# Seven block products instead of eight in twelve tile pairs of the second FFN

## The chip, the cores and the metric

The kernel runs on one core of one Trainium2 chip. The metric is the device time of one execution in microseconds, lower is better. The engines are TensorE (PE, with its weight loads as PEld), VectorE (DVE), ScalarE (ACT), GpSimd (POOL) and SyncE (SP), which issues the transfers. They run in parallel, each through its own queue in the order in which the program is written for it, and meet at semaphores.

## What is computed

A trunk of two layers, 512 tokens of 1024 features: adaptive norm, a mixer (attention in the first layer, a recurrent one in the second), and a gated FFN with a causal convolution of three taps. What matters here is the FFN of the second layer:

```python
def conv_ffn(h, w_up, conv_w, w_down):
    up = causal_dwconv(h @ w_up, conv_w)
    a, b = jnp.split(up, 2, axis=-1)
    return (jax.nn.silu(a) * b) @ w_down

    h = modulate(x, norm_ffn[layer], sh2, sc2)
    x = x + g2[:, None, :] * conv_ffn(h, ffn_w_up[layer], ffn_conv[layer], ffn_w_down[layer])
```

`w_up` is 1024 x 5632 and `w_down` 2816 x 1024, all float32.

## The kernel before

**Layout.** Features lie on the 128 partitions and the 512 tokens along a row. `x` and the normed `h` are eight tiles of 128x512. A float32 operand is split in a high and a low part of the type float32r, and a product is three matmuls (`mm3`, L322 to 326): the weights' high part by the tokens' high part, by their low part, and the weights' low part by the tokens' high part. A 128x128 block of weights is the stationary operand and up to 512 tokens stream past it.

**Weights.** `prep` (L299 to 314) loads one tile of weights (`st`, 512 KB, two buffers) with SyncE, ScalarE casts it to `whi` (L312), VectorE subtracts for `wlo` (L313); `whi` and `wlo` have five buffers each. `weight` (L316 to 320) is called where a product needs its tile, and keeps two tiles of weights prepared ahead (`LA` = 2, L246). The list of all tiles in the order of use is `weight_order`.

**The FFN** (`ffn`, from L510). The 44 feature tiles of the up projection make 22 pairs: tile j (a) and tile 22 + j (b). A pair is 2 x 8 x 3 = 48 matmuls of 128x512 into two PSUM banks that `gbank` (L267 to 269) takes in turn from six. The first two pairs go by halves of the tokens, 256 wide, as the norm's two halves come. `finish` puts the pair through the convolution (`conv`, L516 to 523: one ScalarE operation and two VectorE operations from the bank), Silu, the product and a split into `gh` and `gl`.

**The down projection** sums over the 22 product tiles in three parts (`THIRDS`, L21: 0, 8, 15, 22). After pair 8 and after pair 15 all eight output tiles are made for one part, each 8 or 7 x 3 matmuls, and added to `x` (`residual`, L429). The last part is `out_gemm` (from L483): four tiles 512 wide, then four by halves.

**The norm ahead of it.** `out_gemm` of the mixer, called with a next norm, sums squares (`sq`, `stat`), and `rstd_bc` (L442 to 464) takes their sum over partitions on TensorE (L450), 1 / rms on VectorE by a chain of small operations (`nv`, `nrt`, `nry`, L455 and L351 to 356), and its broadcast on TensorE (L460, bank `t`). `make_h` (L470 to 476) then makes `hu` on VectorE, `hh` on ScalarE and `hl` on VectorE. This runs once per half of the tokens.

The order on each engine comes from the tile framework: code is written in the order above, and a scheduler places each instruction by its priority in the program.

Of the kernel before, what the change touches and what calls it, by code (L numbers as in the profile page):

```python
# [12 lines left out]
ALU = mybir.AluOpType  # L13
# [7 lines left out]
THIRDS = (0, 8, 15, 22)  # L21
# [50 lines left out]
# features of the state space layer: groups of 16 (o) for states of odd and even tiles of states  # L72
# [51 lines left out]
def layout(inp):  # L124
# [55 lines left out]
    dn = np.zeros((2, 3, 8, P, 1024), np.float32)  # L180
    for l in range(2):
        for q in range(3):
            w = wtiles(g["ffn_w_down"][l][THIRDS[q] * P:THIRDS[q + 1] * P])
            dn[l, q, :, :, :w.shape[2]] = w
    A["dn"] = dn
    A["cc"], A["ba"], A["bb"], A["id"], A["turns"], A["i16"] = constants()
    return A


def weight_order():  # L190
# [4 lines left out]
    def ffn(l):  # L195
        r = []
        for j in range(NJ):
            r += [("up", l, j), ("up", l, NJ + j)]
            if j in THIRDS[1:3]:
                r += [("dn", l, THIRDS.index(j) - 1, m) for m in range(8)]  # L200
        return r + [("dn", l, 2, m) for m in range(8)]
# [28 lines left out]
SPLIT_AT = (18, 18, 18, 18)  # L230
REC_K = (2, 3, 4, 5, 0, 1, 6, 7)


class Kernel:
    def __init__(self, nc, tc, I, O, ctx):
        self.nc, self.tc, self.I, self.O, self.ctx = nc, tc, I, O, ctx
        self.guards = {}
# [9 lines left out]
        self.turn = 0  # L247
        self.tturn = 0

# [1 line left out]
    def open(self, name, side="left"):  # L251
        p = self.tc.tile_pool(name=name, bufs=1, side=side, reuse_waits="tile")
        t = p.__enter__()
        self.guards[name] = p
        return t
# [11 lines left out]
    def gbank(self):  # L267
        self.turn = (self.turn + 1) % 6
        return self.bank(("acc", "acc", "s", "s", "o", "o")[self.turn])
# [9 lines left out]
    def source(self, key):  # L279
# [16 lines left out]
        n = (THIRDS[key[2] + 1] - THIRDS[key[2]]) * P  # L296
        return I["dn"][key[1], key[2], key[3], :, :n], n

    def prep(self, pool=None, stage=None):  # L299
        key = self.order[self.next]  # L300
        self.next += 1
        src, n = self.source(key)
# [57 lines left out]
    def ada_first(self, k, pool, V):  # L360
        """Scale and shift of a feature tile of the first norm, in three steps: loads, long sums, last sums."""
# [11 lines left out]
        if k in ADA_PE:  # L373
            # four parts of the sum side by side on the tensor engine
# [67 lines left out]
    def rstd_bc(self, stats, cs, tag="x", warm=None):  # L442
        """1 / rms of each token, on all partitions; stats: squares to be summed."""
# [26 lines left out]
    def make_h(self, l, kind, k, rs, cs):  # L470
        nc = self.nc
        u = self.sp.tile([P, T], F32, name="hu", tag="hu", bufs=2)[:, cs]
# [1047 lines left out]
```

## Time and profile before

| | us |
|---|---|
| median of three runs | 1322.74 (1322.55 to 1324.81) |
| span of the profiled execution | 1321.6 |
| TensorE busy | 1302.3 (99%) |
| weight loads busy | 1075.0 (81%) |
| VectorE busy | 910.8 (69%) |
| ScalarE busy | 576.0 (44%) |

The profiled execution's span is the time from its first to its last recorded instruction; the runs were timed apart. Busy shares are averages over stages with different limits. The second FFN ends the kernel: its first product of full width starts at 976.81, behind two pairs by halves, and the last matmul of the kernel at 1317.84.

### The profile page before, as it was taken

To read this page: it belongs to the slowest core of one execution; us is meant where nothing else is said; L and a number is where in the kernel's file an instruction comes from. 1 tells how busy PE (TensorE), PEld (TensorE's weight loads), DVE (VectorE), ACT (ScalarE), POOL (GpSimd) and SP (SyncE) were. 2 spreads that over 40 slices of the span, in tenths; PEclk is the share of its full clock that TensorE was granted. 3 is DMA by queue.
4 is the path that set the end of the run, shared out by engine and by line. 5 is a ranking of instruction groups with operands and counts; after the bars stand their busy time and mean duration, and the time that the engine had idled before them with its cause. 6 is when DMAs were issued, how large, how long until landed. Compare 5 with 4: busy or idle time off the path is not lost.

```text
span 1321.6 us, 21082 instructions
## 1 busy us (share of the span) xinstructions
PE 1302.3 (99%) x8190; PEld 1075.0 (81%) x8190; DVE 910.8 (69%) x2025; ACT 576.0 (44%) x1114; POOL 3.3 (0%) x11
## 2 busy tenths in 40 slices
PE   8989999999999999999999999999999999999998
PEld 5976776898886888888998879787998888888888
DVE  6986856579995598486678786774885644654652
ACT  4456556445531333233456655553444423432430
POOL 0000000000000000000000000000000000000000
PEclk9999999999999999999999999999999999999999
DMA  9763521516654577363443522311422222222222
GB/s 365 267 224 119 175 65 41 201 65 217 213 170 154 178 252 248 125 212 116 142 159 100 156 92 63 98 31 59 150 97 98 96 96 97 95 94 101 94 79 78
DMA packets 81971, 181.02 MB, mean 137 GB/s; under 512 B 28432, under 2 KB 36048, under 8 KB 81872
## 3 DMA queue, kind: packets, MB, share of 16 engines
q1 hardware_dynamic: 81872, 179.69, 40.4%
q8 instruction: 64, 1.05, 0.3%
q14 instruction: 35, 0.29, 0.1%
HBM read 165.55 MB, written 14.11 MB: 136 GB/s over the span
## 4 chain that ended last, share of the span: by engine, by line
PE 91%; DVE 4%; DMA 2%; ACT 2%; issue 1%; SPq 0%; DVEq 0%; ACTq 0%
PE acc L324 12%; PE acc L325 12%; PE acc L326 12%; PE s L325 7%; PE s L324 7%; PE s L326 7%; PE o L325 7%; PE o L324 7%; PE o L326 6%; PE s L646 3%; PE o L675 2%; DMA ast<-ada 1%; DVE wlo L313 1%; DVE adaj L395 1%; PE t L666 1%
## 5 line engine op out<-in xcount | busy, mean ns | idle before, releaser
L312 ACT CAST whi<-st 128x1024 fp32r<-128x1024 f32 (+1 forms) x196 | 201.1, 1029 | 291.6 <-PE acc L325 101.9
L313 DVE TENSOR_TENSOR wlo<-st,whi 128x1024 fp32r<-128x1024 f32 (+1 forms) x196 | 234.1, 1196 | 127.3 <-ACT whi L312 124.7
L324 PE MATMUL acc<-hh,whi 128*128 128x512 f32 (+1 forms) x488 | 178.9, 370 | 0.9 <-ACT hh L475 0.7
L325 PE MATMUL acc<-hl,whi 128*128 128x512 f32 (+1 forms) x488 | 178.6, 369 | 0.2 <-DVE hl L344 0.2
L326 PE MATMUL acc<-hh,wlo 128*128 128x512 f32 (+1 forms) x488 | 178.0, 367 | 0.0
L325 PE MATMUL s<-hl,whi 128*128 128x512 f32 (+2 forms) x368 | 131.1, 356 | 0.0
L324 PE MATMUL s<-hh,whi 128*128 128x512 f32 (+2 forms) x368 | 130.3, 354 | 0.0
L326 PE MATMUL s<-hh,wlo 128*128 128x512 f32 (+2 forms) x368 | 129.9, 353 | 0.0
L395 DVE CUSTOM_DVE_ANT_0 adaj<-ast,cond 128x1024 bf16<-128x1024 f32 x86 | 104.8, 1218 | 13.8 <-DMA ast<-ada 13.5
L325 PE MATMUL o<-hl,whi 128*128 128x512 f32 (+1 forms) x288 | 106.8, 371 | 0.0
L324 PE MATMUL o<-hh,whi 128*128 128x512 f32 (+1 forms) x288 | 106.7, 370 | 0.0
L326 PE MATMUL o<-hh,wlo 128*128 128x512 f32 (+1 forms) x288 | 106.1, 368 | 0.0
L324 PEld LDWEIGHTS acc<-hh,whi 128*128 128x128 f32 x488 | 91.1, 188 | 17.0 <-ACT hh L475 1.0
L325 PEld LDWEIGHTS acc<-hl,whi 128*128 128x128 f32 x488 | 91.3, 188 | 16.2 <-DVE hl L344 1.2
L326 PEld LDWEIGHTS acc<-hh,wlo 128*128 128x128 f32 x488 | 91.4, 188 | 15.2 <-issue 0.7
L325 PE MATMUL acc<-wlo,hh 128*128 128x256 f32 x320 | 93.3, 292 | 0.0
L324 PE MATMUL acc<-whi,hh 128*128 128x256 f32 x320 | 92.5, 290 | 0.6 <-ACT hh L475 0.6
L326 PE MATMUL acc<-whi,hl 128*128 128x256 f32 x320 | 91.6, 288 | 0.9 <-DVE hl L476 0.9
L324 PEld LDWEIGHTS s<-hh,whi 128*128 128x128 f32 (+1 forms) x368 | 68.3, 186 | 10.8
L326 PEld LDWEIGHTS s<-hh,wlo 128*128 128x128 f32 (+1 forms) x368 | 68.3, 186 | 10.4
L325 PEld LDWEIGHTS s<-hl,whi 128*128 128x128 f32 (+1 forms) x368 | 68.3, 186 | 9.9
L324 PEld LDWEIGHTS acc<-whi,hh 128*128 128x128 f32 x320 | 60.4, 189 | 4.9 <-issue 3.2
(439 smaller groups left out, 2593.5 us busy)
## 6 DMA issues: line engine op xcount, KB each, us to landing
ast<-ada SPq DMA_DIRECT2D x92, 512.0 KB
st<-up SPq DMA_DIRECT2D x88, 512.0 KB
st<-dn SPq DMA_DIRECT2D x32, 448.0 KB
st<-ri SPq DMA_DIRECT2D x20, 512.0 KB
st<-wq SPq DMA_DIRECT2D x17, 512.0 KB
st<-dn SPq DMA_DIRECT2D x16, 512.0 KB
st<-wo SPq DMA_DIRECT2D x8, 512.0 KB
st<-ro SPq DMA_DIRECT2D x8, 512.0 KB
```

The lines of the kernel that those rows point to most:

```text
L312: nc.scalar.copy(hi, st)
L313: nc.vector.tensor_tensor(lo, st, hi.bitcast(F32), ALU.subtract)
L324: mm(out, lh, rh, start=start, stop=False)
L325: mm(out, lh, rl, start=False, stop=False)
L326: mm(out, ll, rh, start=False, stop=stop)
L395: self.nc.vector.tensor_tensor_reduce(junk, st, self.cond, 1.0, 0.0, op0=ALU.mult, op1=ALU.add, accum_out=self.md[l][:, i:i + 1])
L646: nc.tensor.matmul(sb, qT[pr, i * P:(i + 1) * P], kT[pr, j0 * P:(i + 1) * P], start=True, stop=True)
L666: nc.tensor.transpose(tb[:, j * P:(j + 1) * P], ps[par][:, j * P:(j + 1) * P], self.ident)
L675: nc.tensor.matmul(ob[64 * par:64 * par + 64, i * P:(i + 1) * P], V[:, j0 + j, vc:vc + 64], pts[:, par, j * P:(j + 1) * P], start=j == 0, ...
```

## The change

In the second layer's FFN twelve of the 22 pairs (5, 6, 8, 9, 11, 12, 14, 15, 17, 18, 20, 21) are made by Strassen's scheme in Winograd's form. A pair is seen as a 2 x 2 block product: the weights' two feature tiles (a, b) by the two halves of the 1024 inner features, and the tokens' two halves of 256 by the same. Eight block products become seven, each 4 inner tiles x 3 = 12 matmuls of 128x256, 84 in all. Their operands are sums of blocks:

- `prep_pair` loads both tiles of weights of a pair, splits a's two blocks and one of b, makes four sums of blocks on VectorE (128x512) and splits those too: three casts and subtractions of 1024 and one of 512, where two of 1024 were. The buffers `v` have a ring of two.
- `token_sums` makes four sums of the tokens' blocks once, at the entry of the FFN. For that the norm's `hu` tiles are kept (`hk`) and get their shift on ScalarE.
- `seven` makes the products into three banks Z, X, Y, and adds on in PSUM where it can: the order is Z, X, Z, X, Z, Y, Z. Between them ScalarE copies what Z and X held (`p1`, `p7`, `p16`, 128x256) to SBUF, and VectorE and ScalarE make the results `ub` and `ua` there, from which `conv` then reads.

The parts of the down projection in this FFN are (0, 6, 12, 17, 22), four instead of three, and their tiles are spread one or two behind each pair from 6 on (`down_after`). In this FFN the banks go round by eight. `conv` takes its temporaries from the buffers `sq` and `stat`.

```diff
-THIRDS = (0, 8, 15, 22)
+GROUPS = ((0, 8, 15, 22), (0, 6, 12, 17, 22))
+FAST = ((), tuple(j for j in range(4, 22) if j % 3 != 1))
+SPREAD = (False, True)
...
+def down_after(l, j):
+    g = GROUPS[l]
+    q = max(n for n, b in enumerate(g) if b <= j)
+    if q == 0:
+        return []
+    if not SPREAD[l]:
+        return [(q - 1, m) for m in range(8 if j == g[q] else 0)]
+    n, i = g[q + 1] - g[q], j - g[q]
+    return [(q - 1, m) for m in range(8 * i // n, 8 * (i + 1) // n)]
...
+    def prep_pair(self, l, j):
+        pool = (self.wp, self.fp)[j % 2]
+        a, b = (pool.tile([P, 1024], F32, name="st", tag="st", bufs=2) for _ in range(2))
+        nc.sync.dma_start(a, self.I["up"][l, j])
+        nc.sync.dma_start(b, self.I["up"][l, NJ + j])
+        def halves(src, pool, tag, bufs):
+            n = src.shape[1]
+            hi, lo = (pool.tile([P, n], F32R, name=tag + e, tag=tag + e, bufs=bufs) for e in ("hi", "lo"))
+            nc.scalar.copy(hi, src)
+            nc.vector.tensor_tensor(lo, src, hi.bitcast(F32), ALU.subtract)
+            return [(hi[:, c:c + T], lo[:, c:c + T]) for c in range(0, n, T)]
+        f["11"], f["12"] = halves(a, self.wp, "w", 5)
+        f["22"], = halves(b[:, T:], self.fp, "v", 2)
+        a1, a2, b1, b2 = a[:, :T], a[:, T:], b[:, :T], b[:, T:]
+        nc.vector.tensor_tensor(b2, b2, b1, ALU.add)
+        nc.vector.tensor_tensor(b1, b1, a1, ALU.add)
+        nc.vector.tensor_tensor(a1, a1, b2, ALU.add)
+        f["s3"], f["s1"] = halves(b, self.wp, "w", 5)
+        nc.vector.tensor_tensor(a2, a2, a1, ALU.add)
+        f["s2"], f["s4"] = halves(a, self.wp, "w", 5)
...
     def weight(self, key):
-        while self.next < min(ix + (self.LA if ix > 5 else 0) + 1, len(self.order)):
+        ahead = (1 if key[0] == "sp" else self.LA) if ix > 5 else 0
+        if key[0] == "sp" and self.order[min(ix + 1, len(self.order) - 1)][0] == "dn":
+            ahead = 2
+        while self.next < min(ix + ahead + 1, len(self.order)):
...
+    def token_sums(self, l, tp):
+        for k in range(KD):
+            h = self.keep[k]
+            nc.scalar.activation(h, h, AF.Identity, bias=self.shift(l, 1, k))
+        for k in range(4):
+            h, g = self.keep[k], self.keep[k + 4]
+            V_.tensor_tensor(a, h[:, t1], h[:, t2], ALU.subtract)
+            V_.tensor_tensor(c, g[:, t2], h[:, t2], ALU.subtract)
+            V_.scalar_tensor_tensor(b, a, -1.0, g[:, t2], ALU.mult, ALU.subtract)
+            V_.scalar_tensor_tensor(d, b, -1.0, g[:, t1], ALU.mult, ALU.subtract)
+            for e, (n, m) in enumerate((("1", "3"), ("2", "4"))):
+                hi, lo = self.split(s[e], *(tp.tile([P, T], F32R, name=f"b{k}{e}{x}") for x in "hl"))
...
+    def seven(self, f, B, tp):
+        Z, X, Y = (self.gbank()[:, t1] for _ in range(3))
+        def product(acc, a, b, start):
+            for k in range(4):
+                s = slice(k * P, (k + 1) * P)
+                (lh, ll), (rh, rl) = f[a], B[b][k]
+                for n, (x, y) in enumerate(((lh, rh), (lh, rl), (ll, rh))):
+                    nc.tensor.matmul(acc, x[:, s], y, start=start and k == n == 0, stop=k == 3 and n == 2, skip_group_check=not start)
+        product(Z, "11", "11", True)
+        p1 = keep(Z, "p1")
+        product(X, "s3", "3", True)
+        p7 = keep(X, "p7")
+        product(Z, "s2", "2", False)
+        p16 = keep(Z, "p16")
+        product(X, "22", "4", False)
+        V_.scalar_tensor_tensor(v[:, t1], X, -1.0, p16, ALU.mult, ALU.subtract)
+        product(Z, "s1", "1", False)
+        V_.scalar_tensor_tensor(v[:, t2], Z, -1.0, p7, ALU.mult, ALU.subtract)
+        product(Y, "12", "21", True)
+        V_.tensor_tensor(u[:, t1], Y, p1, ALU.add)
+        product(Z, "s4", "22", False)
+        S_.copy(u[:, t2], Z)
```

**TensorE, in pair 8.** In the rows, `o_11022` and `o_11053` are the banks of the pair's two tiles before, `hh` and `hl` the normed tokens, `whi` and `wlo` the weights. Before, at the step from the first tile to the second:

```order
L324 MATMUL o_11022<-hh7_10091,whi_10949 128x512
L325 MATMUL o_11022<-hl7_10092,whi_10949 128x512
L326 MATMUL o_11022<-hh7_10091,wlo_10950 128x512
L324 MATMUL o_11053<-hh0_10077,whi_10980 128x512
L325 MATMUL o_11053<-hl0_10078,whi_10980 128x512
L326 MATMUL o_11053<-hh0_10077,wlo_10981 128x512
```

After, at the step from the second product (X is `o_11277`) to the third, which goes into Z (`o_11276`) again; the `b` tiles are the sums of tokens:

```order
L606 MATMUL o_11277<-b30h_10366,whi_11197 128x256
L606 MATMUL o_11277<-b30l_10367,whi_11197 128x256
L606 MATMUL o_11277<-b30h_10366,wlo_11198 128x256
L606 MATMUL o_11276<-b01h_10328,whi_11202 128x256
L606 MATMUL o_11276<-b01l_10329,whi_11202 128x256
L606 MATMUL o_11276<-b01h_10328,wlo_11203 128x256
```

Where a new bank began, the product now goes on in a bank that held an earlier one, of which ScalarE has taken a copy in between.

**ScalarE, in pair 9.** Before, casts of weights stand between the operations of a pair's convolution and its split; here pair 7 (`s_10946` and `s_10977` are its banks), and it goes on so in all pairs:

```order
L312 CAST whi_11056<-st_11054 128x1024
L520 ACTIVATE ta_11008<-s_10946,pc_70 128x512
L527 ACTIVATE ta_11008<-ta_11008 128x512
L312 CAST whi_11101<-st_11099 128x1024
L520 ACTIVATE tb_11013<-s_10977,pc_70 128x512
L343 CAST gh_11018<-tb_11013 128x512
L312 CAST whi_11133<-st_11131 128x1024
```

After, around the three copies of pair 9 (`acc_11465` is its Z, `s_11466` its X); `vhi_11644` and `st_11637` belong to pair 11, `whi_11436` to a down tile and `whi_11461` to pair 10:

```order
L327 CAST whi_11410<-st_11390 128x1024
L359 CAST whi_11436<-st_11434 128x768
L393 CAST gh_11385<-tb_11380 128x512
L359 CAST whi_11461<-st_11459 128x1024
L610 COPY p1_11482<-acc_11465 128x256
L327 CAST vhi_11644<-st_11637 128x512
L610 COPY p7_11496<-s_11466 128x256
L610 COPY p16_11510<-acc_11465 128x256
L359 CAST whi_11581<-st_11579 128x1024
L650 ACTIVATE tb_11569<-ub_11469,pc_70 128x512
```

The three copies stand among the casts of later weights, one of them behind a cast of a tile of pair 11.

**VectorE, at the entry of the FFN.** The chain of `nv`, `nrt` and `nry` for the second half of the tokens. Before:

```order
L455 TENSOR_SCALAR nv_10261<-x_10258 128x2
L313 TENSOR_TENSOR wlo_10333<-st_10330,whi_10332 128x1024
L351 TENSOR_SCALAR nrt_10264<-nv_10261 128x2
L352 TENSOR_SCALAR nry_10263<-nrt_10264 128x2
L354 TENSOR_TENSOR nrt_10264<-nry_10263 128x2
L355 SCALAR_TENSOR_TENSOR nrt_10264<-nrt_10264,nv_10261 128x2
L356 SCALAR_TENSOR_TENSOR nry_10263<-nrt_10264,nry_10263 128x2
```

After (`vlo_10784` and `st_10776` belong to pair 5):

```order
L505 TENSOR_SCALAR nv_10264<-x_10261 128x2
L328 TENSOR_TENSOR vlo_10784<-st_10776,vhi_10783 128x512
L401 TENSOR_SCALAR nrt_10267<-nv_10264 128x2
L335 TENSOR_TENSOR st_10776<-st_10776 128x512
L402 TENSOR_SCALAR nry_10266<-nrt_10267 128x2
L336 TENSOR_TENSOR st_10776<-st_10776,st_10775 128x512
L404 TENSOR_TENSOR nrt_10267<-nry_10266 128x2
L405 SCALAR_TENSOR_TENSOR nrt_10267<-nrt_10267,nv_10264 128x2
L360 TENSOR_TENSOR wlo_10389<-st_10386,whi_10388 128x1024
L406 SCALAR_TENSOR_TENSOR nry_10266<-nrt_10267,nry_10266 128x2
```

Three operations of 512 of pair 5's weights have moved in between the steps, beside the one subtraction of a weight that stood there.

## Rows read from the trace of the kernel before

**Rows 1.** The page: busy time, share and instructions; chain that ended last.

```profile
PE 1302.3 (99%) x8190; PEld 1075.0 (81%) x8190; DVE 910.8 (69%) x2025; ACT 576.0 (44%) x1114; POOL 3.3 (0%) x11
...
PE 91%; DVE 4%; DMA 2%; ACT 2%; issue 1%; SPq 0%; DVEq 0%; ACTq 0%
```

**Rows 2.** Busy time by window: from:to and length, engines' busy us (instructions), clock, DMA.

```profile
1000.00:1100.00 100.00, 100.00 (x439) 82.05 (x438) 52.84 (x61) 32.05 (x40) 0.00 (x0) 1.00 0.27 95
```

**Rows 3.** Timeline (start, length, engine, line): TensorE's run of full width; the end.

```profile
976.81 0.39 PE L324 MATMUL o<-hh,whi 128*128 128x512 f32 x1
...
1298.17 0.28 PE L324 MATMUL o<-gh,whi 128*128 128x256 f32 x1
...
1317.84 0.28 PE L326 MATMUL acc<-gh,wlo 128*128 128x256 f32 x1
1318.15 0.48 DVE L429 SCALAR_TENSOR_TENSOR x<-acc,mb,x 128x256 f32<-128x256 f32 x1 [1.99 <-PE acc L326]
```

**Rows 4.** Waits from 880 us on (total, times, longest): TensorE's longest; ScalarE's casts.

```profile
PE s L1188 <- DVE z L1183: 0.6, 1, 0.6
...
ACT whi L312 <- PE acc L325: 41.0, 21, 4.4
```

**Rows 5.** A window of 256 wide products only; one group of weight loads from 1298.2 on.

```profile
930.00:940.00 10.00, 10.00 (x87) 10.00 (x86) 7.05 (x12) 4.41 (x7) 0.00 (x0) 1.00 0.44 150
...
L325 PEld LDWEIGHTS o<-gl,whi 128*128 128x128 f32 x28 | 5.3, 188 | 0.0
```

**Rows 6.** Groups of VectorE (count, busy, mean ns): second FFN; last from 880 to 977.

```profile
L313 DVE TENSOR_TENSOR wlo<-st,whi 128x1024 fp32r<-128x1024 f32 x46 | 56.3, 1225 | 56.7 <-ACT whi L312 55.5
L313 DVE TENSOR_TENSOR wlo<-st,whi 128x896 fp32r<-128x896 f32 x16 | 17.4, 1090 | 21.1 <-ACT whi L312 21.1
L529 DVE TENSOR_TENSOR tb<-ta,tb 128x512 f32<-128x512 f32 x21 | 14.5, 692 | 0.8
L521 DVE SCALAR_TENSOR_TENSOR ta<-s,pc,ta 128x511 f32<-128x511 f32 x7 | 5.2, 744 | 0.0
L429 DVE SCALAR_TENSOR_TENSOR x<-acc,mb,x 128x512 f32<-128x512 f32 x8 | 5.9, 750 | 19.7 <-PE acc L326 19.7
...
L429 DVE SCALAR_TENSOR_TENSOR x<-o,mb,x 128x256 f32<-128x256 f32 x4 | 1.9, 480 | 1.4 <-PE o L326 1.4
```

**Rows 7.** Groups of ScalarE: second FFN; the last one, a copy from PSUM, whole kernel.

```profile
L312 ACT CAST whi<-st 128x1024 fp32r<-128x1024 f32 x45 | 47.1, 1048 | 81.3 <-PE acc L325 27.8 <-PE s L325 27.4 <-PE o L325 22.3
L343 ACT CAST gh<-tb 128x512 fp32r<-128x512 f32 x22 | 13.7, 620 | 56.2 <-DVE tb L529 56.2
L520 ACT ACTIVATE tb<-s,pc 128x512 f32<-128x512 f32 x8 | 5.5, 685 | 0.0
...
L667 ACT COPY PT<-x 128x256 f32<-128x256 f32 x16 | 6.0, 373 | 5.7 <-PE x L666 5.5
```

**Rows 8.** One load of weights: SyncE's issue, then windows with the DMA share.

```profile
1045.03 0.33 SPq L309 DMA_DIRECT2D st<-dn  x1
...
1045.75:1046.00 0.25, 0.25 (x3) 0.21 (x2) 0.25 (x1) 0.00 (x0) 0.00 (x0) 1.00 0.10 16
...
1047.75:1048.00 0.25, 0.25 (x3) 0.19 (x2) 0.14 (x1) 0.08 (x1) 0.00 (x0) 1.00 0.31 82
```

**Rows 9.** Timeline of VectorE: the chain to 1 / rms of the second half.

```profile
958.24 0.16 DVE L455 TENSOR_SCALAR nv<-x 128x2 f32<-128x2 f32 x1
958.32 1.21 DVE L313 TENSOR_TENSOR wlo<-st,whi 128x1024 fp32r<-128x1024 f32 x1
959.45 0.16 DVE L351 TENSOR_SCALAR nrt<-nv 128x2 int32<-128x2 int32 x1
...
961.41 0.16 DVE L356 SCALAR_TENSOR_TENSOR nry<-nrt,nry 128x2 f32<-128x2 f32 x1
```

**Rows 10.** Timeline behind it: TensorE's broadcast; ScalarE's hh, two tiles a row.

```profile
961.80 0.60 PE L460 MATMUL t<-ident,nry 128*128 128x128 f32 x4
...
962.96 0.91 ACT L475 ACTIVATE hh<-hu,mb 128x256 fp32r<-128x256 f32 x2 [5.43 <-DVE hu L474]
...
964.81 0.91 ACT L475 ACTIVATE hh<-hu,mb 128x256 fp32r<-128x256 f32 x2 [0.94 <-DVE hu L474]
```

More of the change, by code (lines that the diff above doesn't have):

```diff
@@ L197, in ffn @@
         for j in range(NJ):
[L198 to L201, printed above, removed]
+            r += [("sp", l, j)] if j in FAST[l] else [("up", l, j), ("up", l, NJ + j)]
+            r += [("dn", l, q, m) for q, m in down_after(l, j)]
+        return r + [("dn", l, len(GROUPS[l]) - 2, m) for m in range(8)]
     o += ffn(0)
@@ L254, in open @@
         self.guards[name] = p
+        self.guarded[name] = t
         return t
@@ L301, in prep @@
         self.next += 1
+        if key[0] == "sp":
+            self.ready[key] = self.prep_pair(*key[1:])
+            return
         src, n = self.source(key)
@@ new lines, in seven, with keep @@
+    def seven(self, f, B, tp):
+        nc = self.nc
+        V_, S_ = nc.vector, nc.scalar
+        t1, t2 = slice(0, 256), slice(256, T)
+        Z, X, Y = (self.gbank()[:, t1] for _ in range(3))
+        u, v = (self.sp.tile([P, T], F32, name=n, tag="hu", bufs=2) for n in ("ua", "ub"))
+        def product(acc, a, b, start):
[4 more added lines that the diff above has]
+                    nc.tensor.matmul(acc, x[:, s], y, start=start and k == n == 0, stop=k == 3 and n == 2, skip_group_check=not start)
+        def keep(acc, nm):
+            t = tp.tile([P, 256], F32, name=nm, tag=nm, bufs=2 if nm == "p1" else 1)
+            S_.copy(t, acc)
+            return t
+        product(Z, "11", "11", True)
[12 more added lines that the diff above has]
+        S_.copy(u[:, t2], Z)
+        return u, v
@@ L512, in ffn @@
         lo, hi = slice(0, 256), slice(256, T)
-        gp, tp = self.open(f"fg{l}", "right"), self.open(f"ft{l}", "right")
+        fast = bool(FAST[l])
+        g = GROUPS[l]
+        self.turns = 8 if fast else 6
+        if not fast:
+            self.open(f"fg{l}", "right")
+        gp, tp = self.guarded[f"fg{l}"], self.open(f"ft{l}", "right")
         if True:
             G = {}
+            if fast:
+                self.fp = tp
+                B = self.token_sums(l, tp)
             def conv(acc, c, tag):
-                t = tp.tile([P, T], F32, name="t" + tag, tag="t" + tag, bufs=2)
+                if fast:
+                    t = self.sp.tile([P, T], F32, name="t" + tag, tag={"a": "sq", "b": "stat"}[tag], bufs=1)
+                else:
+                    t = tp.tile([P, T], F32, name="t" + tag, tag="t" + tag, bufs=2)
                 o = 132 * l + 3 * c
@@ L529, in finish @@
                 nc.vector.tensor_tensor(b, a, b, ALU.mult)
-                G[j] = self.split(b, *(gp.tile([P, T], F32R, name="g" + s, tag="g" + s, bufs=10) for s in "hl"))
+                G[j] = self.split(b, *(gp.tile([P, T], F32R, name="g" + s, tag="g" + s, bufs=12 if fast else 10) for s in "hl"))
             w = [self.weight(("up", l, c)) for c in (0, NJ, 1, NJ + 1)]
@@ L537, in ffn @@
             for j in range(NJ):
-                if j < 2:
+                if j in FAST[l]:
+                    aa, bb = self.seven(self.weight(("sp", l, j)), B, tp)
+                elif j < 2:
                     aa, bb = accs[2 * j], accs[2 * j + 1]
```

62 lines of the change are left out of this document (41 added, 21 removed).

## The prediction

> **What bounds the kernel now.** I read the page first. TensorE is busy 99% of the span and makes 91% of the chain that ended last [rows 1]. Then the stretch of the second FFN: in 100 us of it TensorE has no idle time at all, VectorE is busy 53% and ScalarE 32%, the weight loads 82%, the clock is granted in full, the DMA engines are used to 27% [rows 2]. So this stretch lasts as long as its matmuls do, and only two things can change its length: their number and pitch, or a new wait that lets TensorE run dry. The pitch comes from starts of matmuls: 1404 products of 128x512 start between 976.81 and 1298.17, which is 0.2289 us each; 168 of 128x256 lie between 1298.17 and the last start at 1317.84, which is 19.67 / 167 = 0.1178 us each [rows 3]. (1404 is counted in the code: 20 pairs x 48, 8 tiles x 24, 8 x 21, and 4 x 21 of the last third.) The list of waits has nothing of this stretch for TensorE; its longest sum after 880 us is 0.6 us, and that is before the second FFN [rows 4].
>
> **What the products give.** A pair now: 48 x 0.2289 = 10.99 us. A pair by seven products: 7 x 4 x 3 = 84 matmuls of 128x256, 84 x 0.1178 = 9.90 us. The gain is 1.09 us, not an eighth of 10.99 (1.37), since a narrow matmul costs 0.1178 and not half of 0.2289. Twelve pairs: 13.1 us. The down projection keeps its products; its last group has five operands instead of seven, so 24 matmuls of 512 are added and 48 of 256 go: 24 x 0.2289 - 48 x 0.1178 = -0.16 us.
>
> At that width the array's other side is full: where 256 wide matmuls run, the loads of weights are busy 10.00 us of 10, at 512 wide 82% [rows 2, 5]; one load's record is 188 ns long, more than the pitch, so the records overlap [rows 5]. The row has this price in the pitch already. A rule that speaks against the change stands in the Trainium skill, TensorE: Matmul & The Clock Gate, Part 3 (the mechanism of packing): a load of weights overlaps matmuls in flight only when it goes to other rows of the array, and its section on LDWEIGHTS puts a load of 128 rows at P / 1.2 ns, 107 ns; every load here takes all rows, so by that page, as an estimate, the 36 more loads of a pair would cost 3.9 us and the pair would lose. By this trace they don't: 0.1178 us holds load and matmul together.
>
> **What feeds the seven products.** Each pair's staging grows. VectorE: three subtractions of 1024 (1.225 us) and one of 512 (0.69), four sums (0.69), three results of 256 (0.48 at most), with the convolution's 4 x 0.745, the product and the split 0.69 each [rows 6]: 12.9 us, against 6.8 for a plain pair. Two fast pairs and a plain one, with four to five down tiles (a subtraction of 768, some 0.95 between the rows of 512 and 896, and a sum of 0.75): 40 us, or 36 as the records overlap by 0.08, in 48 to 49 us of TensorE. ScalarE: three casts of 1.05, one of 0.62, four copies of 0.37, the convolution's part 2.6 (two of 0.685, two of 0.62) [rows 7]: 7.9 us for a fast pair, 24 of 48 over three. Neither becomes the bound on average, so I put this at nothing; the cover is the idle half of ScalarE and quarter of VectorE.
>
> What is new on TensorE's path is the order inside a pair: Z, X, Z, X, Z, Y, Z. The third product adds into Z, so it waits until ScalarE has copied p1 out of it; the fourth likewise for p7, the fifth for p16, and the last for VectorE's second half of ub. Between the end of a product in Z and the next one into it lies one other product, 12 x 0.1178 = 1.41 us (for ub: the product into Y). Out of that go the last matmul's result (its record is 0.28 us, 0.16 past the next start [rows 3]), the copy at 0.37 [rows 7] or the sum at 0.48 [rows 6], and two hand-overs of 0.03 (the last matmul's record ends at 1318.12, VectorE starts at 1318.15 [rows 3]): about 0.65. So each of 12 x 4 releases can stand 0.75 us behind other work in its queue before TensorE waits. A cast of 1024 that has just started takes 0.97 before the next can go, so it costs 0.2 us; two in a row 1.2. I worked each queue through pair by pair in the order in which it is written, with these durations: every copy comes in time, but by 0.05 to 0.4 us in pairs 6, 15 and 18, and by 0.8 in pair 9, where a cast that waits for a transfer stands between p1 and p7. There the load goes out when VectorE is done with its stage's last reader; a load of 448 KB issued at 1045.03 moves its bytes from 1045.9 to 1047.95 [rows 8], 2.9 us. From below this is nothing (a copy can't bring more than no wait); from above 36 copies x 0.2 = 7 us. Hand times are not exact to 0.1 us, so I take 0.9 us, nearer the bottom, since ScalarE is busy half of the time and most copies meet a free queue.
>
> **The entry.** The sums of tokens (8 ScalarE operations and 8 casts, 16 short VectorE operations and 8 subtractions, 10 and 13 us) need both halves of the tokens and are first read in pair 5, three plain pairs (33 us) later; the 11 us of products by halves and the first plain tiles cover them. But VectorE's order before them changes. The chain of small operations to 1/rms of the second half has one subtraction of a weight inside it now and takes from 958.24 to 961.57; its steps go every 0.195 us, and the one with the subtraction takes 1.21 [rows 9]. After the change three operations of 512 stand in it as well, about 0.48 more each: 4.8 us instead of 3.3. TensorE has 41 matmuls between the sum of squares and the broadcast (31 before): 10 x 0.118 = 1.2 us of the 1.5 are covered. After the broadcast only 10 matmuls are left, 1.2 us, where 26 were, and from the broadcast's start at 961.80 the first hh is ready after 962.96 + 0.5, 1.7 us [rows 10]; with 0.36 for the broadcast itself 0.1 to 0.3 is open. Together 0.4 to 0.6, and up to as much again while the norm's tiles, two in 1.85 us [rows 10], are waited for. Bounds: 0 (the covers hold) and 2.0 (1.5 with no cover, and 0.5 behind the broadcast); I take 0.9, nearer to the single gaps worked out. Right after it the weight of the second plain tile is subtracted behind the sums, ready within 0.3 us of its use.
>
> **The rest.** Eight more down loads of equal bytes in all: DMA at 27% [rows 2]. SP's queue only stands longer for stages. The residual adds are counted above. Eight banks go round instead of six, so the convolutions that the sums hold up don't hold the banks. The end is the same: last matmul at 1317.84, an add, the store [rows 3].
>
> **The sum.** Span 1321.6 - 13.1 - 0.16 + 0.9 (entry) + 0.9 (copies) = 1310.1. The runs' median lies 1.1 us above this span (1322.74 against 1321.6), so 1311.2; I say 1311.
>
> **The rivals.**
> (a) ScalarE's copies are late all over, by one cast each: 36 x 0.2 to 0.4 us = 7 to 14 more, 1317 to 1323. For it: casts of weights waited for TensorE to free a slot, behind the acc banks' products alone 41.0 us in 21 times and up to 4.4 [rows 4], and a copy behind such a cast waits too. Against: those waits end at matmuls that come earlier in TensorE's own order.
> (b) Slower than before: in each fast pair one copy stands behind a cast whose transfer comes late. One costs up to 2.9 + 0.62 + 0.65 - 1.41 = 2.8 us. From 1.28 us a pair on (15.3 / 12) the kernel is slower by over 0.2%; at 2.8 in all twelve it gives 1311 - 0.9 + 33 = 1344. For it: pair 9 has that order. Against: only pairs 9 and 12 have a transfer so near, with 0.8 us left.
> (c) The whole gain with no new wait: 1321.6 - 13.3 + 1.1 = 1309.5.
> (d) The loads of weights stop overlapping in the new rhythm: 36 more loads a pair at up to their record's 0.188 us [rows 5], 81 us, 1392. That is what the page named above would give by the trace's own duration; the trace speaks against it at the same width and the same order of operands.
>
> **How the numbers follow.** Forecast (1309.5 to 1314): 0.62. Case (a): 0.20, of which 0.16 under 1320. Case (c), 1308.5 to 1309.5: 0.09. Case (b): 0.05, (d): 0.01. Something in between, with no change that can be told: 0.03. A measurement tells about 0.2%, 2.6 us, from no change. Faster: 0.62 + 0.16 + 0.09 = 0.87; same: 0.04 + 0.03 = 0.07; slower: 0.06. The range from 1308.5 to 1317 leaves out most of (a), (b) and (d), about 0.2.
>
> **What would show it.** Right: 1008 matmuls of 128x256 in the fast pairs at 0.118 us, 9.9 us from a pair's first to its last; TensorE's waits for ScalarE's copies together under 2 us, for ub near none; the run of 512 wide products starting 0.5 to 1.5 us later than 976.81. Wrong: a pitch above 0.12 in fast pairs (loads), TensorE waiting on p1, p7 or p16 in every pair (a), on a cast whose releaser is a DMA (b), or for a wlo (VectorE the bound, against my 36 of 48).

## The result, and the profile after

The changed kernel takes 1309.3 us (median of four runs, 1308.51 to 1311.11), the kernel before 1323.26 us in the runs beside it. The ratio is 0.9893, with a 95% interval of 0.9879 to 0.9907: 14 us less, 1.1% faster; the interval leaves out 1. Forecast were 1311 us and a range of 1308.5 to 1317. The profiled execution has a span of 1306.9 us, 14.7 less than before.

The page: TensorE is still the bound, with 408 more matmuls in 14 us less; the two engines that prepare its operands are busier [rows 1].

```profile
PE 1288.2 (99%) x8598; PEld 1082.0 (83%) x8598; DVE 984.3 (75%) x2173; ACT 621.9 (48%) x1210; POOL 3.6 (0%) x11
...
PE 88%; DVE 5%; DMA 3%; ACT 2%; issue 1%; SPq 0%; DVEq 0%; ACTq 0%
```

Windows of the second FFN (from:to and length, busy us of PE, PEld, DVE, ACT with counts, clock, DMA share), to be read against [rows 2]: TensorE has lost 0.16 and 0.28 us in 100, VectorE has gone from 53% to 83 and 75%, ScalarE from 32% to 52 and 47%.

```profile
1000.00:1100.00 100.00, 99.84 (x620) 89.31 (x619) 83.09 (x116) 51.85 (x80) 0.00 (x0) 1.00 0.30 101
1100.00:1200.00 100.00, 99.72 (x593) 87.97 (x591) 74.86 (x104) 47.05 (x69) 0.00 (x0) 1.00 0.30 103
```

The timeline of TensorE (start, length, engine, line) at the first products of full width, through pair 9, and at the end:

```profile
966.72 0.40 PE L374 MATMUL o<-hh,whi 128*128 128x512 f32 x1
...
977.79 0.40 PE L375 MATMUL o<-hl,whi 128*128 128x512 f32 x1
...
1067.53 0.28 PE L606 MATMUL acc<-hh,whi 128*128 128x256 f32 x1
...
1071.61 0.28 PE L606 MATMUL s<-b01h,vhi 128*128 128x256 f32 x1
...
1073.05 0.28 PE L606 MATMUL acc<-b00h,whi 128*128 128x256 f32 x1
...
1077.13 0.39 PE L374 MATMUL o<-gh,whi 128*128 128x512 f32 x1
...
1289.68 0.28 PE L374 MATMUL o<-gh,whi 128*128 128x256 f32 x1
...
1303.16 0.28 PE L376 MATMUL acc<-gh,wlo 128*128 128x256 f32 x1
```

Three things are read from it. The stretch from the start of the run of full-width products to the last matmul takes 1303.16 - 977.79 = 325.37 us, where 1317.84 - 976.81 = 341.03 stood before [rows 3]: 15.66 us less. The run starts 0.98 us later, of which 0.41 was there already at the first half's sum of squares (942.30 against 941.89), in code that the change leaves alone. And one product of full width, at 966.72, no longer belongs to the run: it stands among the halves ahead of it and takes 0.24 us there, so the stretch holds one product of about 0.23 us less than before. Pair 9 takes 1077.13 - 1067.53 = 9.60 us: its fourth product, with the `v` weights, takes 1.44 us, 0.120 a matmul, and the other six have 8.16 us for 72, 0.1133. The halves at the end go at 13.48 / 119 = 0.1133 too, where 0.1178 was measured before.

The stretch is the better scale for small differences. The changed kernel, profiled again on another occasion, gave 325.35 us (run after_again, below), while spans moved by 2 us from run to run, and the first half's sum of squares, ahead of what the runs change, came anywhere from 941.5 to 947.7 us.

By terms, in us, with all twelve pairs read from the timeline as the time from a pair's first matmul to the next tile's first (117.06 in all):

| term | predicted | measured |
|---|---|---|
| twelve pairs without waits | -13.1 | 12 x (9.60 - 10.987) = -16.6 |
| waits in the pairs, and the pitch behind them | +0.9 | 117.06 - 115.2 = +1.9 |
| the last group | -0.16 | -0.7 |
| entry of the FFN | +0.9 | +0.57 |
| the product of full width that went into the entry, out of the stretch | 0 | -0.23 |
| ahead of the change | 0 | +0.4 |
| sum | -11.5 | -14.7 |

Of the 1.9 us, 1.0 are four waits ahead of a product (pairs 6, 11, 15 and 18). Another 0.55 are five single steps of 0.22 us instead of 0.11, four of them right behind these waits and one in pair 8. The rest is pitch: 0.1178 through the first three products of pair 5, and behind the waits.

### The profile page after: what moved, and what is told of

Same layout as the page of the kernel before. It is cut to its first block, busy times and chain, and to the rows that moved or that the text cites. A ratio compares the mean times of both kernels' runs of the same rounds, so it can differ in the third digit from the quotient of the medians.

```text
span 1306.9 us, 22172 instructions
## 1 busy us (share of the span) xinstructions
PE 1288.2 (99%) x8598; PEld 1082.0 (83%) x8598; DVE 984.3 (75%) x2173; ACT 621.9 (48%) x1210; POOL 3.6 (0%) x11
## 4 chain that ended last, share of the span: by engine, by line
PE 88%; DVE 5%; DMA 3%; ACT 2%; issue 1%; SPq 0%; DVEq 0%; ACTq 0%
PE acc L374 10%; PE acc L375 10%; PE acc L376 10%; PE s L375 5%; PE s L376 5%; PE s L374 5%; PE o L375 5%; PE o L376 5%; PE o L374 5%; PE s L776 3%; PE o L805 2%; PE s L606 2%; PE o L606 2%; PE t L606 2%; DMA ast<-ada 1%
## 5 line engine op out<-in xcount | busy, mean ns | idle before, releaser
L359 ACT CAST whi<-st 128x1024 fp32r<-128x1024 f32 (+3 forms) x180 | 177.8, 991 | 231.8 <-PE acc L375 73.4
L360 DVE TENSOR_TENSOR wlo<-st,whi 128x1024 fp32r<-128x1024 f32 (+3 forms) x180 | 206.1, 1147 | 57.8 <-ACT whi L359 56.1
L445 DVE CUSTOM_DVE_ANT_0 adaj<-ast,cond 128x1024 bf16<-128x1024 f32 x86 | 105.1, 1222 | 13.1 <-DMA ast<-ada 12.9
L375 PE MATMUL s<-hl,whi 128*128 128x512 f32 (+2 forms) x280 | 96.1, 344 | 0.0
L376 PE MATMUL s<-hh,wlo 128*128 128x512 f32 (+2 forms) x280 | 96.0, 343 | 0.0
L374 PE MATMUL s<-hh,whi 128*128 128x512 f32 (+2 forms) x280 | 95.5, 342 | 0.0
L374 PE MATMUL o<-hh,whi 128*128 128x512 f32 (+1 forms) x208 | 75.2, 362 | 0.0
L375 PE MATMUL o<-hl,whi 128*128 128x512 f32 (+1 forms) x208 | 75.2, 361 | 0.0
L375 PEld LDWEIGHTS acc<-wlo,hh 128*128 128x128 f32 x320 | 60.9, 190 | 3.9 <-issue 3.7
L376 PEld LDWEIGHTS acc<-whi,hl 128*128 128x128 f32 x320 | 60.6, 190 | 4.0 <-issue 2.3
L327 ACT CAST whi<-st 128x1024 fp32r<-128x1024 f32 x36 | 37.7, 1049 | 48.3 <-PE o L375 8.1
```

Of the source, the lines that this page charges most:

```text
L327: nc.scalar.copy(hi, src)
L359: nc.scalar.copy(hi, st)
L360: nc.vector.tensor_tensor(lo, st, hi.bitcast(F32), ALU.subtract)
L374: mm(out, lh, rh, start=start, stop=False)
L375: mm(out, lh, rl, start=False, stop=False)
L376: mm(out, ll, rh, start=False, stop=stop)
```

## The experiments

Besides the time, each run is judged by the stretch just named: 341.03 us in the kernel before, 325.37 in the changed one. The entry is the time from the first half's sum of squares on TensorE to the run of wide products: 34.92 and 35.49 us. In the runs below where pair 5's or pair 4's staging is put later, in the last one, and in the two without fast pairs, no wide product stands in the entry, so their stretch holds 0.23 us more work than that of the others.

### Eight products in narrow form

```diff
-FAST = ((), tuple(j for j in range(4, 22) if j % 3 != 1))
+FAST = ((), ())
+HALF = tuple(j for j in range(4, 22) if j % 3 != 1)
...
-                B = self.token_sums(l, tp)
...
+                    parts = (lo, hi) if l == 1 and j in HALF else (slice(0, T),)
...
+                    for cs in parts:
+                        self.gemm(aa, wa, self.h, cs)
...
+                    for cs in parts:
+                        self.gemm(bb, wb, self.h, cs)
```

> The twelve pairs are made by all eight block products, 96 matmuls of 128x256 in two plain banks, with plain weights and no sums of tokens or of weights; the four groups of the down projection, their spreading and the eight banks stay as in the changed kernel. Theory (the gain is the seventh product that is left out, and a narrow product costs no more per column than a wide one): a pair takes 96 x 0.1133 = 10.88 us, so the kernel stands near 1322, 12 to 13 us above the changed one. With a pitch of 0.1178, as the prediction took it, a pair takes 11.31 us and the kernel is at 1326 to 1327. Rival (the gain comes from the spread down projection and the banks): near 1310.

1329.55 us, ratio 1.0035 (1.0023 to 1.0048): slower than before, which took 1324.44 us beside it. Stretch 344.71 us, entry 34.95, as before. The timeline of TensorE through one pair:

```profile
1051.44 0.28 PE L375 MATMUL s<-hh,whi 128*128 128x256 f32 x1
...
1062.75 0.39 PE L375 MATMUL o<-gh,whi 128*128 128x512 f32 x1
```

96 matmuls in 11.31 us, 0.1178 each, and so in all twelve pairs; 12 x (11.31 - 10.99) - 0.16 = 3.7 us above the kernel before, as measured. So without the scheme the narrow form loses, and neither the spreading nor the banks bring the gain. From here to the changed kernel it is 19.3 us: twelve products less in each pair are 12 x 12 x 0.1178 = 17.0, and the rest is the better pitch and the wide product in the entry, less the waits. The time is above both numbers of the expectation. Of the two pitches that the expectation named, the larger one held here by the stretch, so my theory that a narrow product costs nothing more was wrong for this kernel.

### The spread down projection alone

```diff
-FAST = ((), tuple(j for j in range(4, 22) if j % 3 != 1))
+FAST = ((), ())
+HALF = ()
...
-                B = self.token_sums(l, tp)
```

> No fast pairs at all: 22 plain pairs of 128x512, with the four groups, the spreading and the eight banks of the changed kernel. Theory: TensorE never waited in this stretch, so the new order of the down tiles brings nothing but the last group's shorter halves, 0.2 to 0.7 us: 1322.5. Rival (the order and the banks bring the gain): near 1310.

1324.72 us, ratio 1.000 (0.999 to 1.001). Stretch 340.89 us, 0.14 less than before: the prediction's -0.16 for the last group, since the halves at the end go at 0.1178 here. TensorE had nothing to win from the order.

### Each copy twice

```diff
             S_.copy(t, acc)
+            S_.copy(t, acc)
             return t
```

> Each copy of p1, p7 and p16 is made twice into the same buffer, 0.37 us more of ScalarE ahead of each of 36 releases. Theory (a release has some 0.75 us to spare, less where another operation stands ahead of it): only the pairs that wait already (5, 6, 8, 15, 18) and a few more lose, 6 to 10 copies x 0.3, so 2 to 3 us more than the changed kernel: 1311 to 1312.5. Rival (no release has anything to spare, ScalarE is the bound): 36 x 0.37 = 13 us more, 1322.

1312.81 us, ratio 0.9908 (0.9893 to 0.9923). Stretch 327.70 us, 2.33 more than the changed kernel. The waits of TensorE (us in total, times, longest); first the changed kernel's list for the second FFN, then this one's:

```profile
PE acc L606 <- DVE ub L622: 0.2, 1, 0.2
PE t L606 <- ACT p L610: 0.2, 1, 0.2
```

```profile
PE acc L606 <- DVE ub L623: 0.9, 1, 0.9
PE acc L606 <- ACT p L611: 0.5, 1, 0.5
PE t L606 <- ACT p L611: 0.3, 1, 0.3
```

So 36 x 0.37 = 13 us of ScalarE work in front of the releases cost 2.3, within the theory's 2 to 3 (the time is 0.3 above its range): the spare time that the prediction worked out for each copy is there, in most pairs.

### Casts behind the copies

What the changed kernel waits for is seen in pair 6. ScalarE, then TensorE:

```profile
1022.25 0.36 ACT L610 COPY p<-o 128x256 f32<-128x256 f32 x1
1023.31 1.06 ACT L359 CAST whi<-st 128x1024 fp32r<-128x1024 f32 x1 [0.71 <-DMA st<-up]
1024.27 0.36 ACT L610 COPY p<-t 128x256 f32<-128x256 f32 x1
...
1024.25 0.28 PE L606 MATMUL o<-b31h,wlo 128*128 128x256 f32 x1
1024.68 0.38 PE L606 MATMUL t<-b01h,vhi 128*128 128x256 f32 x1 [0.15 <-ACT p L610]
```

The second product (bank `t`) ended with the last matmul ahead of 1023.0, whose record ends at 1023.17, but its copy p7 stands behind a cast that waited 0.71 us for a transfer. It starts at 1024.27, and TensorE, done at 1024.25 but for the pitch, goes on at 1024.68, 0.3 us late. In pair 15 it is p1, behind a cast that waited 0.72 us for a transfer; in pairs 8 and 18 p1 stands behind the cast of a `gh`. The experiment puts the casts that are prepared in a fast pair behind its last copy (`self.kept` is the copy of p16). The call that prepares stands there in the program too, so the loads and VectorE's part of the preparation come later as well:

```diff
+        with self.tc.issue_after(self.kept.ins):
+            self.prep_now(pool, stage)
...
         p16 = keep(Z, "p16")
+        while self.next < self.upto:
+            self.prep()
```

> ScalarE's casts of weights that are prepared during a fast pair are put behind that pair's copy of p16 in ScalarE's queue. Theory (TensorE's waits for p1 and p7 in pairs 5, 6, 8, 15 and 18 come from a cast, or an operation behind one, that stands ahead of the copy): these waits go, 1.4 us in all, pitch as before, so the span falls to about 1305.5 and the time to 1308. Rival (the copies are late for want of ScalarE's time, whatever their order, or the casts are then late for the tiles that follow): no change or more, 1309.3 or above, with new waits for wlo in front of down tiles.

1310.97 us, ratio 0.9903 (0.9886 to 0.9920). Stretch 327.35 us, 1.98 more than the changed kernel: the rival's side, though by waits for `ub` and not for `wlo`. Pair 12 is the dearest; ScalarE, VectorE and TensorE there:

```profile
1121.56 1.05 ACT L365 CAST whi<-st 128x1024 fp32r<-128x1024 f32 x1 [2.48 <-DMA st<-up]
...
1122.64 1.23 DVE L366 TENSOR_TENSOR wlo<-st,whi 128x1024 fp32r<-128x1024 f32 x1 [2.00 <-ACT whi L365]
1123.79 0.42 DVE L631 SCALAR_TENSOR_TENSOR ub<-o,p 128x256 f32<-128x256 f32 x1
...
1124.26 0.38 PE L613 MATMUL o<-hh,whi 128*128 128x256 f32 x1 [1.21 <-DVE ub L631]
```

The wait has moved: the cast comes late, VectorE's subtraction for the same weight comes late with it, and `ub`, which the last product waits for, now stands behind that subtraction. The cast is late for its transfer: SyncE issues that load at 1117.04, 2.8 us behind the pair's first product, where it goes out 0.25 us behind it in the changed kernel (1114.95). No product waits for a copy any more, so the copies were late because of their order, as I thought. But what helps ScalarE here delays VectorE, and nothing is won by it. Whether the casts' order alone would do that, without the later loads, this run can't tell.

### Pair 5's staging behind the norm

The entry in the changed kernel, VectorE then TensorE, against [rows 9, 10]:

```profile
959.32 0.16 DVE L505 TENSOR_SCALAR nv<-x 128x2 f32<-128x2 f32 x1 [0.76 <-PE x L500]
959.40 0.69 DVE L328 TENSOR_TENSOR vlo<-st,vhi 128x512 fp32r<-128x512 f32 x1
960.01 0.16 DVE L401 TENSOR_SCALAR nrt<-nv 128x2 int32<-128x2 int32 x1
...
964.04 0.16 DVE L406 SCALAR_TENSOR_TENSOR nry<-nrt,nry 128x2 f32<-128x2 f32 x1
...
964.35 0.35 PE L510 MATMUL t<-ident,nry 128*128 128x128 f32 x1
```

The chain takes 4.88 us (4.8 predicted, 3.33 before), and the broadcast starts 0.41 us after the matmul ahead of it (963.94), 0.29 more than the pitch; before, it followed after 0.12 (961.68 to 961.80). With the 0.24 us of the wide product at 966.72 that is 0.53 of the entry's 0.57 us.

```diff
+            if key[2] == FAST[1][0]:
+                with self.tc.issue_after(self.last.ins):
+                    self.ready[key] = self.prep_pair(*key[1:])
```

> VectorE's part of pair 5's staging is put behind the last operation of the norm in VectorE's queue; nothing else is changed. Theory (the three operations of 512 inside the chain to 1 / rms make the entry longer by 0.57 us): the chain takes 3.3 us again, the broadcast comes without a wait, and the stretch from the second sum over partitions to the first wide run is 0.3 to 0.6 us shorter than in the changed kernel, 1309 in all. Rival (the entry is longer because the tiles x5 to x7 are updated later): no change.

1310.65 us, ratio 0.9883 (0.9856 to 0.9911). The entry is 35.19 us, 0.30 less than in the changed kernel, and the stretch the same, 325.38. The chain in this kernel:

```profile
961.16 0.16 DVE L509 TENSOR_SCALAR nv<-x 128x2 f32<-128x2 f32 x1 [0.76 <-PE x L504]
...
963.33 0.16 DVE L410 SCALAR_TENSOR_TENSOR nry<-nrt,nry 128x2 f32<-128x2 f32 x1
```

From 961.16 to 963.33 + 0.16: 2.33 us instead of 4.88, since the other subtraction left the chain as well. But TensorE still waits, 0.44 us ahead of the broadcast, as that one now stands behind 18 matmuls and not 41. And 0.24 of the 0.30 us are the wide product, which has gone back into the run; without it the entry is 34.92 us before, 35.25 in the changed kernel and 35.19 here. So a shorter chain gave the entry 0.06 us at most, and the theory isn't borne out. From the first half's sum to the last matmul it is 360.57 us against 360.86, and where these 0.29 us come from is not shown. The times can't tell 0.3 us.

### Down tiles in one piece

```diff
-SPREAD = (False, True)
+SPREAD = (False, False)
```

> The twelve fast pairs stay, but the eight down tiles of a group are made in one piece at pairs 6, 12 and 17, and not one or two behind each pair. Theory (the spread down tiles give VectorE and ScalarE time between fast pairs): two fast pairs and a plain one give TensorE 2 x 9.6 + 11 = 30.2 us and VectorE some 29.5 with overlaps, with more in the fast pairs than in the plain one, so TensorE waits 1 to 2 us in each such three: 1313 to 1318. Rival (the two weights prepared ahead even this out, and the spreading does nothing): 1309 to 1310.

1310.6 us, ratio 0.9892 (0.9867 to 0.9916); stretch 326.75 us. The rival is right: the spreading is worth at most 1.4 us, of which the halves at the end, here at 0.1177 again, are 0.5. The windows of pairs 5 and 6, which stand next to each other, and of the eight down tiles and the plain pair 7 behind them:

```profile
1013.80:1032.90 19.10, 19.10 (x169) 19.10 (x168) 17.56 (x28) 13.44 (x23) 0.00 (x0) 1.00 0.24 84
1033.00:1076.80 43.80, 43.80 (x194) 35.96 (x193) 28.24 (x37) 14.30 (x18) 0.00 (x0) 1.00 0.31 108
```

VectorE is busy 92% in the two pairs and 64% in the piece behind them, and TensorE 100% in both. I had taken VectorE's whole work of a pair as due within the pair. By the code only the copies, `ub` and the next weights are; the convolution and the split of a fast pair may wait in their buffers until the down tiles give VectorE time, in one piece as well as spread.

### Seventeen fast pairs

```diff
-FAST = ((), tuple(j for j in range(4, 22) if j % 3 != 1))
+FAST = ((), tuple(range(5, 22)))
```

> All pairs from 5 to 21 by seven products, 17 instead of 12. Theory: each further pair gives 1.2 to 1.4 us of TensorE, 6 to 7 in all, against more waits for ub and the copies, since VectorE then has some 14 us of work for 16 of TensorE a pair with its down tiles, 88%: 2 to 5 us of waits, so 1304 to 1308. Rival (VectorE becomes the bound as soon as fast pairs stand without a plain one between): 1309 or more, with TensorE waiting for wlo in most pairs.

1306.57 us, ratio 0.986 (0.9838 to 0.9882). Stretch 323.28 us, 2.09 less than with twelve. Five more pairs at 10.99 - 9.60 would be 6.9, so 4.8 us went into waits. Where, by the list of TensorE's waits and a window of pairs 5 to 8:

```profile
PE x L606 <- DVE ub L622: 0.9, 1, 0.9
PE s L606 <- DVE ub L622: 0.6, 1, 0.6
PE t L606 <- DVE ub L622: 0.6, 1, 0.6
PE s L606 <- ACT p L610: 0.4, 1, 0.4
...
1009.70:1058.00 48.30, 47.77 (x372) 45.30 (x371) 44.49 (x67) 30.70 (x50) 0.00 (x0) 1.00 0.29 96
```

With VectorE at 92% over 48 us most of the waits are for `ub`, a short operation, and none for `wlo`. In pairs 9, 17 and 19, the dearest without a down tile between their products, `ub` stands behind operations of 0.7 us for later weights. That speaks for VectorE's order as the trouble, with its amount nearly so; no run tries another order. The rival's 1309 and waits for `wlo` didn't come.

### Sixteen, in two ways, and seventeen with the later staging

```diff
-FAST = ((), tuple(j for j in range(4, 22) if j % 3 != 1))
+FAST = ((), tuple(j for j in range(5, 22) if j != 7))
```

Beside this edit the staging of the first fast pair stands behind the norm, as above; so it does in the next one and in the last.

> Pairs 5 to 21 by seven products but for pair 7 (16), with pair 5's staging behind the norm. With 17, pairs 6 and 7 lost 2.9 and 3.5 us against 84 x 0.1133 = 9.52, pair 9 1.7, 17 and 19 1.4 each, where few down tiles stand behind a pair; the others lost 0.1 to 0.4. Theory (VectorE and ScalarE fall behind in three fast pairs in a row without down tiles, 5 to 7): with pair 7 plain those 6.3 us go but for 0.5, at a cost of 10.99 - 9.6 = 1.4: the stretch from the first wide run to the last matmul is 318.5 to 320 us (323.3 with 17, 325.4 in the changed kernel), the time near 1303. Rival (the losses move to the pairs behind, as the work of staging is the same): 322 or more, 1306.

1308.24 us, ratio 0.9874 (0.9860 to 0.9888); stretch 324.33 us, 1.05 more than with 17 (0.23 of it the wide product): the rival's side. The expectation rested on a misreading of mine: the 2.9 and 3.5 us that pairs 6 and 7 seemed to lose with 17 hold the matmuls of a down tile, which the scheduler had put between the products (ten of them from 1027.91 to 1030.19 in the kernel with 17). Without them the two lost 0.5 and 1.3 us, so there was little to win back, and a plain pair costs 1.4. Pairs 9, 17 and 19 lose 1.2 to 1.6 us each here as with 17.

```diff
-FAST = ((), tuple(j for j in range(4, 22) if j % 3 != 1))
+FAST = ((), tuple(j for j in range(4, 22) if j not in (6, 7)))
```

> Pairs 4, 5 and 8 to 21 by seven products (16), 6 and 7 plain, pair 4's staging behind the norm. By the same theory the first two fast pairs then stand ahead of two plain ones and lose 0.5 each, but their staging meets VectorE's backlog of the sums of tokens: stretch 319 to 321 us. By the rival (the staging's sum decides) 322 or more.

1311.64 us, ratio 0.9901 (0.9887 to 0.9915); stretch 326.63 us, the rival's side again. Pair 4 alone takes 12.91 us here, with steps of 0.5 to 1.0 us from one matmul to the next between 1002.8 and 1007.4, where TensorE waits for pair 4's own weights: the longest ends with a `wlo` that VectorE makes from 1003.48 to 1004.71. The expectation's reason, a backlog of the sums of tokens, isn't it: the last of these ends at 981.3. VectorE begins pair 4's staging only at 998.14; why so late is not shown.

The changed kernel itself, on the same chip:

> The changed kernel itself, on this chip, for comparison with the two others: stretch 325.4 us, time within 0.2% of 0.989 of the kernel before.

1310.12 us, ratio 0.9888 (0.9871 to 0.9905); stretch 325.35 us.

Last, the 17 pairs, `tuple(range(5, 22))`, with the later staging:

> Pairs 5 to 21 by seven products (17), with pair 5's staging behind the norm: the two changes that gave something, together. From the second layer's first sum over partitions to the last matmul 358.7 us with 17 pairs alone and 360.6 with the later staging alone, against 360.8 in the changed kernel. Theory (the parts don't touch one another): 358.4 to 358.6, about 0.986 of the kernel before. Rival (the staging that is put later falls on pairs 5 to 7, which have nothing to spare in a row): 359 or more.

1307.33 us, ratio 0.9883 (0.9861 to 0.9904). From the first half's sum of squares to the last matmul 358.92 us, against 358.73 with 17 pairs alone and 360.8 in the changed kernel: the later staging gives nothing on top, and the time lies between theory and rival. By this scale 17 pairs are 2 us better than 12, and better than both kernels; the intervals of the times overlap, so the times alone don't show it.

### The fourth product's weights in the common ring

```diff
-            hi, lo = (pool.tile([P, n], F32R, name=tag + e, tag=tag + e, bufs=bufs) for e in ("hi", "lo"))
+            hi, lo = (pool.tile([P, 1024], F32R, name=tag + e, tag=tag + e, bufs=bufs)[:, :n] for e in ("hi", "lo"))
...
-        f["22"], = halves(b[:, T:], self.fp, "v", 2)
+        f["22"], = halves(b[:, T:], self.wp, "w", 5)
```

> The block of weights of the fourth product lies in the ring of the other weights (tiles of 1024 columns, half of it used), not in its own small ring; the products are the same. The ring of five then turns faster, so there will be more waits, and the time is not what is asked. Asked is the pitch: in the changed kernel the fourth product goes at 0.120 us a matmul and the others at 0.1133, and pairs that begin or wait at 0.1178 change to 0.1133 behind the fourth. Theory (it is the place of these tiles): the fourth product goes as the others do, and no change of pitch stands behind it. Rival (it is the sequence of products and waits): 0.120 in the fourth as before.

1312.77 us in one run; stretch 328.05 us, with waits of 1.4 us and less, as the ring of five turns faster. The pitch, in pair 8 on TensorE (start of the first product, of the fourth, and of the tile behind the pair):

```profile
1051.51 0.28 PE L606 MATMUL o<-hh,whi 128*128 128x256 f32 x1
...
1055.59 0.28 PE L606 MATMUL o<-b01h,whi 128*128 128x256 f32 x1
...
1061.03 0.39 PE L374 MATMUL x<-gh,whi 128*128 128x512 f32 x1
```

9.52 us for 84, 0.1133 in all of them, the fourth included (1055.59 to 1056.95 is 1.36 us). So the 0.120 belongs to the `v` tiles; whether to their place or to their size of 512 columns isn't separated. The other half of the theory held as well: behind the fourth product no pair changes its pitch unless there is a wait. Pair 5 ran at 0.1178 throughout, pair 15 too, behind a wait of 0.2 us at the end of pair 14, and pair 17 for its first 72 products. At waits the pitch still changes between 0.1178 and 0.1133.

## Why the prediction was right, point by point

**What bounds the kernel.** Right: TensorE was and is the bound, and the gain is one of matmuls. Eight products in the same narrow form are slower than before by 3.7 us of the stretch; leaving out the eighth is what pays.

**The gain of a pair** is the term that was mis-sized. I took 0.1178 us for a narrow product, the only value that the last 20 us of the kernel before show [rows 3], and got 1.09 us a pair. In the changed kernel most products go at 0.1133, and a pair without waits gains 10.99 - 9.60 = 1.39. That is 3.5 us in twelve pairs and 0.5 us at the end. So the sign of being right that I had named, 9.9 us a pair at 0.118, did not come. The 0.1178 was not wrong as a reading: with eight products it held. That the same instructions have two pitches was to be seen in the trace of before, had I looked at all narrow runs. The first layer's FFN ends with the same products by halves; the first run of them there, 97 products, by the starts of its first and last:

```profile
638.31 0.28 PE L324 MATMUL o<-gh,whi 128*128 128x256 f32 x1
...
649.19 0.28 PE L324 MATMUL o<-gh,whi 128*128 128x256 f32 x1
```

10.88 / 96 = 0.1133. What makes the difference is open, so about 4 of the 14.7 us come from a pitch whose cause no run shows.

**Loads of weights.** Right: the rule of the Trainium skill (TensorE: Matmul & The Clock Gate, Part 3) would have made the change lose. 0.1133 us hold a load of all rows and a matmul of 256 columns in this trace, so the loads overlap. (The prediction's 107 ns hold for this load, but in that section of the Trainium skill P counts a load's columns, not its rows; both are 128 here.)

**Waits in a pair.** The mechanism was right and the size half of what came: 0.9 taken, 1.9 measured, with the slower pitch behind a wait counted in. The pairs named as close, 6, 15 and 18, are three of those that waited (10.02, 10.03 and 9.82 us against 9.60); pairs 5 and 8 lost 0.15 and 0.17. Pair 11, which I had not named, took 10.09; there the last product waits for `ub`, which stands behind two operations of VectorE for the next pair's weights. VectorE, then TensorE:

```profile
1103.12 0.69 DVE L328 TENSOR_TENSOR vlo<-st,vhi 128x512 fp32r<-128x512 f32 x1 [0.54 <-ACT vhi L327]
1103.85 0.69 DVE L335 TENSOR_TENSOR st<-st 128x512 f32<-128x512 f32 x1
1104.46 0.42 DVE L622 SCALAR_TENSOR_TENSOR ub<-acc,p 128x256 f32<-128x256 f32 x1
...
1104.93 0.39 PE L606 MATMUL acc<-hh,whi 128*128 128x256 f32 x1 [0.17 <-DVE ub L622]
```

Pair 9, which I had named too, came through without a wait.

**Staging.** Right that neither engine becomes the bound; VectorE's 75% stands in the second window above. But my account of why was too strict: the spread down tiles are not what makes room, as the run in one piece showed.

**The entry.** 0.9 taken, 0.57 measured, of which 0.24 is work out of the stretch. The chain was as worked out (4.88 against 4.8), and so was its cover: 0.3 left open by the sum, 0.29 measured ahead of the broadcast. What came to less is the part behind the broadcast, where no step from one start to the next is longer than 0.24 us.

**From span to time.** I added 1.1 us, the distance between a median and the span of one other execution. The changed kernel's profiled run has both numbers: 1309.07 us and a span of 1306.9, so 2.2. With the right distance the forecast would have been 1312.3; the pitch and the waits brought it to 1309.3. That 1311 came within 1.7 us is thus partly luck: the change of the span was forecast 3.2 us too small, and a distance 1.1 us too short hid a part of it.

**Rivals.** (a), (b) and (d) didn't come as a time. The mechanism of (b), a copy behind a cast whose transfer comes late, did come in pairs 6 and 15, at 0.4 us a pair and not at 2.8. (c), 1309.5, is nearest to the time by number, but not by its reason, since waits did come and the larger gain of a pair paid for them.

## What to carry to other kernels

A scheme that trades one matmul in eight for additions pays when TensorE has no idle time and the other engines have, and its gain is to be reckoned at the pitch of the narrower product: look at every run of that shape in the trace, not at one, and keep both ends. In a pipeline of such products, what counts on the other engines is, beside their load, the few short operations that release the next product and what stands ahead of them in their queues; to put one engine's work later can hurt the next one, as the casts behind the copies did here. Of work that is prepared ahead, ask what is due when: only that part needs the room.

## What the runs showed of the hardware

A product of 128x256 has three main pitches in these traces, with the granted clock at 1.00 throughout: 0.1133 us, 0.1178, and 0.120. (Others occur: 0.1183 from 930 to 941 us, before and after.) The first two come with the same instructions on the same data. One run of 109 such products in the first layer, far ahead of anything the change touches, by the starts of its first and its last in TensorE's timeline, before and then after:

```profile
253.94 0.28 PE L324 MATMUL o<-hh,whi 128*128 128x256 f32 x1
...
266.66 0.28 PE L324 MATMUL o<-hh,whi 128*128 128x256 f32 x1
```

```profile
254.95 0.28 PE L374 MATMUL o<-hh,whi 128*128 128x256 f32 x1
...
267.19 0.28 PE L374 MATMUL o<-hh,whi 128*128 128x256 f32 x1
```

12.72 / 108 = 0.1178 before and 12.24 / 108 = 0.1133 after. The pitch seems to be a state that lasts: with eight products, where TensorE never waits, it stays at 0.1178 from the entry to the last matmul, through all stretches of wide products. It changes at waits, in either direction, but not only there. In the changed kernel it falls from 0.1183 to 0.1133 at 953.39 from one product to the next, with no wait between; and pair 11's last product goes at 0.1178 behind its wait, pair 12's first at 0.1133, with 36 wide products and no wait between. Behind the products whose weights lie in the `v` tiles it was 0.1133, up to the next wait, in all pairs of the changed kernel, though not in every pair of the other runs. Those products go at 0.120 themselves, and in pair 8 at 0.1133 from the other ring. What the state is, and how a program could choose it, is open; no run here settles it. It is worth 0.0045 us a product, 4.5 us in this kernel's twelve pairs, more than all waits.
